# Splitting a weight tile into its two parts by DMAs in a two-block transformer kernel

## The chip, the cores and the metric

The kernel runs on one core of a Trainium2 chip. The metric is device time in microseconds, the lower the better. Below, PE is the matrix engine, DVE the vector engine, ACT the scalar engine, POOL the GpSimd engine and SP the engine that only starts DMAs and handles semaphores.

## The reference

512 tokens of width 1024 pass through two blocks in float32. The first block projects the normalised input with one wide matrix into an attention branch (8 heads, 2 key heads) and a bidirectional gated delta-rule branch (8 heads, chunks of the sequence one after the other), mixes both, and adds a gated embedding. The second block has two layers, one with stick-breaking attention and one with differential attention, each followed by a feed-forward part of width 2816:

```python
g = jnp.einsum('bsd,df->bsf', h, w_gate)
u = jnp.einsum('bsd,df->bsf', h, w_up)
return jnp.einsum('bsf,fd->bsd', jax.nn.silu(g) * u, w_down)
```

What matters here is that every weight matrix is read once and multiplied with all 512 tokens.

## The kernel before, in words

A float32 product would be slow on PE, so each operand is split into two float32r numbers: `hi`, the operand rounded to float32r, and `lo`, what is left, rounded as well. A product is then three float32r matmuls, hi by hi, hi by lo and lo by hi (`mm3`, L307). A weight tile has 128 partitions of 1024 numbers, 512 KB (768 numbers for the last third of `w_down`). It serves eight blocks of 128 rows of the reduction, so a tile is worth 24 matmuls of 512 columns (`proj_fm`, L364), or 48 of 256 columns for the projections that keep tokens on partitions (`proj_tm`, L381).

`wtile` (L322) makes the two parts. SP loads the tile into a staging buffer `st` (L327), of which there are WST = 2. ACT casts it into `whi` and DVE subtracts that from `st` into `wlo` (`split`, L317 and L320). There are WHI = 3 and WLO = 3 buffers for the parts, and from the second block on one more pair, `w3`, which every fourth tile takes (L329). A buffer comes free when PE has used its tile, a staging buffer when DVE has subtracted. In all 295 tiles go through `wtile`. 16 half tiles go another way, `wtile_big` (L335): POOL's queue loads them, and ACT and DVE split them.

The order of the work is made in two steps. A driver (L97) runs Python generators, streams such as the projections and the attention heads, against a clock of estimated times and so fixes the order in which instructions are written down. A scheduler of the framework then orders them for each engine; instructions inside `high_priority(offset=...)` (L325, offset 200) may go ahead of others by as many places. Each engine works its own queue in order, and an instruction that waits for a semaphore holds what is behind it. POOL's queue holds its arithmetic (rsqrt by a power in `small_rsqrt`, L1836, masks, clearing of tiles) and any DMA that it starts.

The rest stays as it is: two PSUM banks `acc` for the projections, five `z` for attention, one `o`.

Of the kernel before, what the change touches and what calls it, by code (L numbers as in the profile page):

```python
# [9 lines left out]
F32 = mybir.dt.float32  # L10
F32R = mybir.dt.float32r
I32 = mybir.dt.int32
AF = mybir.ActivationFunctionType
ALU = mybir.AluOpType
# [3 lines left out]
P = 128  # L18
# [29 lines left out]
CH2 = 1.3  # L48
CH3 = 1.3
INV_SLOW = 1.7  # L50
WST = 2
WHI = 3
WLO = 3
INV_LAT = 8.0
POOLS = dict(big=57, tmp=9, sm=4)
POOLS1 = dict(hf=12, lb=1)
# [23 lines left out]
class Event:  # L80
    def __init__(self):
        self.t = None
# [85 lines left out]
class Net:  # L168
    def __init__(self, ctx, tc, ins, out):
        self.tc = tc  # L170
        self.nc = tc.nc
        self.ins = ins
        self.out = out
        self.drv = Driver()
        self.pre = None
        self.nw = 0

        self.wnext = []
        self.woff = WOFF
        self.w3 = None  # L180

        self.hold = None
        pool = lambda name, bufs, **k: ctx.enter_context(tc.tile_pool(name=name, bufs=bufs, **k))
        self.cp = pool("consts", 1)
        self.wst = pool("wst", WST)
        self.whi = pool("whi", WHI)
        self.wlo = pool("wlo", WLO)
        self.xp = pool("xp", 8)
        self.dp = pool("dp", 2, space=bass.MemoryType.DRAM)
        self.ps = {"acc": pool("acc", 2, space=PSUM), "z": pool("z", 5, space=PSUM), "o": pool("o", 1, space=PSUM)}  # L190
        self.free = {"acc": Slots(2), "z": Slots(5), "o": Slots(1), "e": Slots(E_SLOTS)}
        self.preload_ln()
        self.fv = self.cp.tile([P, self.ins["fvec"].shape[1]], F32, name="fv")
        with self.tc.high_priority(offset=1000):
            self.nc.sync.dma_start(out=self.fv, in_=self.ins["fvec"])
        self.ones = self.cp.tile([P, P], F32, name="ones")
        self.nc.gpsimd.memset(self.ones, 1.0)
        self.eps1 = self.cp.tile([P, 2], F32, name="eps1")
        self.nc.gpsimd.memset(self.eps1[:, 0:1], EPS)
        self.nc.gpsimd.memset(self.eps1[:, 1:2], 4 * EPS)  # L200
        self.mhalf = self.cp.tile([P, 64], F32, name="mhalf")
        self.nc.gpsimd.memset(self.mhalf, -0.5)
        self.rfm = self.cp.tile([P, T], F32, name="rfm")
        self.rt = self.cp.tile([P, 4], F32, name="rt")
# [117 lines left out]
    def wtile(self, ap, n=1024):  # L322

        nc = self.nc
        with self.tc.high_priority(offset=self.woff):  # L325
            st = self.wst.tile([P, 1024], F32, tag="st", name="st")
            nc.sync.dma_start(out=st[:, :n], in_=ap)  # L327
            self.nw += 1
            third = self.w3 is not None and self.nw % 4 == 0  # L329
            hi = (self.w3 if third else self.whi).tile([P, 1024], F32R, tag="hi", name="whi")  # L330
            lo = (self.w3 if third else self.wlo).tile([P, 1024], F32R, tag="lo", name="wlo")
            self.split(hi[:, :n], lo[:, :n], st[:, :n])
        return hi, lo

    def wtile_big(self, ap):  # L335
# [1846 lines left out]
```

## Time and profile before

| | us |
|---|---|
| median of 3 runs (2175.8 to 2181.85) | 2178.52 |
| the profiled execution | 2179.57 |
| its span, first to last instruction | 2177.9 |
| PE busy in the span | 2101.2 |
| DVE busy | 1231.3 |
| ACT busy | 1000.5 |
| POOL busy | 117.0 |

Busy times are of one execution. Issuing a DMA isn't counted as busy. A group of instructions has a line of the code, an engine, an operation, the names of its output and inputs, a count, its busy time, the mean of one in ns, and after the bar the idle time of its engine just before, with what ended it ("issue": nothing that the profile shows). A row of DMA issues gives the size and the time from issue to landing.

### The profile page before, as it was taken

Reading aid. Unit: us, or ns where it says so; the run is one execution under the profiler, and the core shown is the slowest. Engines: PE = TensorE matmul, PEld = TensorE weight load, DVE = VectorE, ACT = ScalarE, POOL = GpSimd, SP = SyncE. Lnnn points to the kernel's source line nnn. Section 1 sums busy time; section 2 is a strip of 40 time slices with the busy share of each in tenths; the row PEclk is TensorE's granted clock in tenths of the full one; section 3 lists DMA queues with packets and bytes.
Section 4 is the critical chain, followed back from the end, with each engine's and each line's share of the span. In section 5 each row is a group of like instructions: output and inputs, shape, how many; then the busy total and the mean of one; then the engine's idle time right before and its main releaser. Section 6 shows DMA issues by size and latency. Waiting matters only on the chain.

```text
span 2177.9 us, 33391 instructions
## 1 busy us (share of the span) xinstructions
PE 2101.2 (96%) x13214; PEld 1804.9 (83%) x13214; DVE 1231.3 (57%) x2519; ACT 1000.5 (46%) x2015; POOL 117.0 (5%) x157
## 2 busy tenths in 40 slices
PE   7999999989999999899999999999999989999999
PEld 6798888879788877788878888888999878888887
DVE  8865865886542546855555444433577765444421
ACT  6556647555622355666664222222465643222211
POOL 2000110100000000000000000000111100000000
PEclk9999999999999999999999999999999999999999
DMA  4221121222334443011112222333211112333332
GB/s 154 73 81 50 46 75 50 62 78 62 103 105 142 148 153 107 14 46 59 53 45 97 97 95 95 91 95 99 88 59 51 52 54 97 97 97 96 92 110 71
DMA packets 73996, 181.72 MB, mean 83 GB/s; under 512 B 24176, under 2 KB 24816, under 8 KB 73840
## 3 DMA queue, kind: packets, MB, share of 16 engines
q1 hardware_dynamic: 72560, 175.40, 25.3%
q0 software_dynamic: 1280, 4.20, 0.6%
q8 instruction: 104, 1.70, 0.3%
q14 instruction: 52, 0.43, 0.1%
HBM read 170.13 MB, written 9.44 MB: 82 GB/s over the span
## 4 chain that ended last, share of the span: by engine, by line
PE 79%; DVE 11%; ACT 5%; issue 2%; POOL 2%; DMA 1%; SPq 0%; POOLq 0%; DVEq 0%; ACTq 0%
PE pg L301 17%; PE pd L301 11%; PE pu L301 11%; PE po L301 8%; PE pb L301 4%; PE z L301 3%; PE pv L301 3%; PE pz L301 3%; PE wS L301 2%; PE pk L301 2%; DVE wlo L320 2%; DVE cacc L845 2%; PE sb_q L301 2%; PE sb_k L301 1%; PE s L301 1%
## 5 line engine op out<-in xcount | busy, mean ns | idle before, releaser
L317 ACT CAST whi<-st 128x1024 fp32r<-128x1024 f32 (+1 forms) x295 | 305.8, 1039 | 796.1 <-issue 331.6
L320 DVE TENSOR_TENSOR wlo<-st,whi 128x1024 fp32r<-128x1024 f32 (+1 forms) x295 | 356.3, 1209 | 279.7 <-ACT whi L317 275.6
L301 PE MATMUL pg<-rlo,whi 128*128 128x512 f32 x352 | 138.7, 394 | 0.0
L301 PE MATMUL pg<-rhi,whi 128*128 128x512 f32 x352 | 138.1, 392 | 0.0
L301 PE MATMUL pg<-rhi,wlo 128*128 128x512 f32 x352 | 137.9, 392 | 0.0
L301 PE MATMUL pd<-mh,wlo 128*128 128x512 f32 x352 | 137.5, 391 | 0.0
L301 PE MATMUL pd<-mh,whi 128*128 128x512 f32 x352 | 137.5, 391 | 0.0
L301 PE MATMUL pd<-ml,whi 128*128 128x512 f32 x352 | 137.5, 391 | 0.0
L301 PE MATMUL pu<-rhi,wlo 128*128 128x512 f32 x352 | 137.2, 390 | 0.0
L301 PE MATMUL pu<-rlo,whi 128*128 128x512 f32 x352 | 137.1, 389 | 0.0
L301 PE MATMUL pu<-rhi,whi 128*128 128x512 f32 x352 | 137.0, 389 | 0.0
L2050 DVE TENSOR_TENSOR sg<-pg,rfm 128x512 f32<-128x512 f32 x44 | 30.4, 692 | 118.2 <-PE pg L301 118.1
L2056 DVE TENSOR_TENSOR m<-pu,sg 128x512 f32<-128x512 f32 x44 | 30.4, 692 | 115.4 <-PE pu L301 115.4
L301 PE MATMUL pv<-whi,rhi 128*128 128x256 f32 x256 | 75.9, 297 | 3.3 <-ACT tmq L1868 2.1
L301 PEld LDWEIGHTS pg<-rhi,wlo 128*128 128x128 f32 x352 | 66.2, 188 | 15.1 <-issue 0.5
L301 PEld LDWEIGHTS pg<-rlo,whi 128*128 128x128 f32 x352 | 66.3, 188 | 15.0 <-issue 0.5
L301 PEld LDWEIGHTS pg<-rhi,whi 128*128 128x128 f32 x352 | 66.2, 188 | 14.5
L301 PEld LDWEIGHTS pd<-ml,whi 128*128 128x128 f32 x352 | 66.2, 188 | 14.3
L301 PEld LDWEIGHTS pd<-mh,wlo 128*128 128x128 f32 x352 | 66.1, 188 | 14.3
L301 PEld LDWEIGHTS pd<-mh,whi 128*128 128x128 f32 x352 | 66.1, 188 | 14.2
L301 PEld LDWEIGHTS pu<-rhi,whi 128*128 128x128 f32 x352 | 66.1, 188 | 14.0
L301 PEld LDWEIGHTS pu<-rlo,whi 128*128 128x128 f32 x352 | 66.1, 188 | 14.0
(563 smaller groups left out, 5820.8 us busy)
## 6 DMA issues: line engine op xcount, KB each, us to landing
st<-w_gate SPq DMA_DIRECT2D x44, 512.0 KB, 3.4
st<-w_up SPq DMA_DIRECT2D x44, 512.0 KB, 3.5
st<-w_down SPq DMA_DIRECT2D x32, 512.0 KB, 3.6
st<-w_dn SPq DMA_DIRECT2D x24, 512.0 KB, 3.6
st<-w_out SPq DMA_DIRECT2D x24, 512.0 KB, 3.5
st<-w_down SPq DMA_DIRECT2D x16, 384.0 KB, 3.1
x<-xT SPq DMA_DIRECT2D x16, 256.0 KB, 6.5
st<-w_aq SPq DMA_DIRECT2D x8, 512.0 KB, 3.6
```

The costliest lines, as they stand in the source:

```text
L301: self.nc.tensor.matmul(out, lhsT=lhsT, rhs=rhs, start=start, stop=stop, skip_group_check=True)
L317: nc.scalar.copy(hi, src)
L320: nc.vector.tensor_tensor(lo, src, hi.bitcast(F32), op=ALU.subtract)
L845: nc.vector.scalar_tensor_tensor(out=acc[:, a], in0=raw[:, b], scalar=w[:, s:s + 1], in1=acc[:, a], op0=ALU.mult, op1=ALU.add)
L2050: nc.vector.tensor_tensor(sg, ps, self.rfm, op=ALU.mult)
L2056: nc.vector.tensor_tensor(m, ps, sg, op=ALU.mult)
```

## The change

The staging buffers and the load into them go. POOL's queue starts a DMA straight from DRAM into `hi`, which is float32r, so the DMA rounds. ACT then writes the negative of `hi` into `lo`, and a second DMA on POOL's queue adds the same weights from DRAM to what is in `lo`. DVE has no part in it, and SP issues no weight load of `wtile` any more. The buffers are now 4 for each part, and every fifth tile takes the extra pair in the second block.

```diff
--- before.py
+++ after.py
@@ -48,9 +48,8 @@
 CH2 = 1.3
 CH3 = 1.3
 INV_SLOW = 1.7
-WST = 2
-WHI = 3
-WLO = 3
+WHI = 4
+WLO = 4
 INV_LAT = 8.0
 POOLS = dict(big=57, tmp=9, sm=4)
 POOLS1 = dict(hf=12, lb=1)
@@ -182,7 +181,6 @@
         self.hold = None
         pool = lambda name, bufs, **k: ctx.enter_context(tc.tile_pool(name=name, bufs=bufs, **k))
         self.cp = pool("consts", 1)
-        self.wst = pool("wst", WST)
         self.whi = pool("whi", WHI)
         self.wlo = pool("wlo", WLO)
         self.xp = pool("xp", 8)
@@ -323,13 +321,14 @@
 
         nc = self.nc
         with self.tc.high_priority(offset=self.woff):
-            st = self.wst.tile([P, 1024], F32, tag="st", name="st")
-            nc.sync.dma_start(out=st[:, :n], in_=ap)
             self.nw += 1
-            third = self.w3 is not None and self.nw % 4 == 0
-            hi = (self.w3 if third else self.whi).tile([P, 1024], F32R, tag="hi", name="whi")
-            lo = (self.w3 if third else self.wlo).tile([P, 1024], F32R, tag="lo", name="wlo")
-            self.split(hi[:, :n], lo[:, :n], st[:, :n])
+            extra = self.w3 is not None and self.nw % (WHI + 1) == 0
+            hi = (self.w3 if extra else self.whi).tile([P, 1024], F32R, tag="hi", name="whi")
+            lo = (self.w3 if extra else self.wlo).tile([P, 1024], F32R, tag="lo", name="wlo")
+
+            nc.gpsimd.dma_start(out=hi[:, :n], in_=ap)
+            nc.scalar.mul(lo[:, :n], hi[:, :n].bitcast(F32), -1.0)
+            nc.gpsimd.dma_start(out=lo[:, :n], in_=ap, accum_op=ALU.add)
         return hi, lo
 
     def wtile_big(self, ap):
```

## Rows read from the trace of the kernel before

**Rows 1.** The page, busy us per engine (share of the span) and instructions

```profile
PE 2101.2 (96%) x13214; PEld 1804.9 (83%) x13214; DVE 1231.3 (57%) x2519; ACT 1000.5 (46%) x2015; POOL 117.0 (5%) x157
```

**Rows 2.** The page, the chain that ended last: by engine, by line

```profile
PE 79%; DVE 11%; ACT 5%; issue 2%; POOL 2%; DMA 1%; SPq 0%; POOLq 0%; DVEq 0%; ACTq 0%
PE pg L301 17%; PE pd L301 11%; PE pu L301 11%; PE po L301 8%; PE pb L301 4%; PE z L301 3%; PE pv L301 3%; PE pz L301 3%; PE wS L301 2%; PE pk L301 2%; DVE wlo L320 2%; DVE cacc L845 2%; PE sb_q L301 2%; PE sb_k L301 1%; PE s L301 1%
```

**Rows 3.** Windows: length, busy us of PE, PEld, DVE, ACT, POOL; clock, DMA share, GB/s

```profile
400.00:545.00 145.00, 135.11 (x1419) 122.83 (x1419) 113.88 (x285) 81.88 (x227) 9.30 (x9) 0.95 0.25 73
...
605.00:760.00 155.00, 155.00 (x689) 128.35 (x688) 62.02 (x82) 48.34 (x75) 3.30 (x4) 1.00 0.40 135
...
1170.00:1412.00 242.00, 242.00 (x1060) 198.56 (x1059) 113.75 (x138) 72.48 (x93) 0.00 (x0) 1.00 0.30 95
...
1532.00:1775.00 243.00, 224.90 (x1732) 214.65 (x1730) 177.97 (x598) 139.94 (x284) 43.76 (x41) 0.98 0.18 57
```

**Rows 4.** The chain in order of time: start, length, what

```profile
1181.53 5.44 PE pg L301 x24
```

**Rows 5.** The page, costliest groups: busy us, mean ns | idle before, releaser

```profile
L317 ACT CAST whi<-st 128x1024 fp32r<-128x1024 f32 (+1 forms) x295 | 305.8, 1039 | 796.1 <-issue 331.6
L320 DVE TENSOR_TENSOR wlo<-st,whi 128x1024 fp32r<-128x1024 f32 (+1 forms) x295 | 356.3, 1209 | 279.7 <-ACT whi L317 275.6
```

**Rows 6.** Timeline, 1230 to 1237 us: start, length, engine, line [idle before]

```profile
1230.68 1.05 ACT L317 CAST whi<-st 128x1024 fp32r<-128x1024 f32 x1 [3.87 <-issue]
...
1231.77 1.23 DVE L320 TENSOR_TENSOR wlo<-st,whi 128x1024 fp32r<-128x1024 f32 x1 [0.21 <-ACT whi L317]
...
1233.02 0.33 SPq L327 DMA_DIRECT2D st<-w_gate  x1
...
1236.12 1.05 ACT L317 CAST whi<-st 128x1024 fp32r<-128x1024 f32 x1 [3.86 <-issue]
```

**Rows 7.** Waits of SP's queue and of PE: us in total, times, longest

```profile
SPq L327 <- DVE wlo L320: 1540.9, 267, 48.9
...
PE ab L301 <- ACT whi L317: 6.7, 1, 6.7
```

**Rows 8.** The tile wbst: its loads from POOL, ns min/median/max, first and last start

```profile
L342 POOL DMA_DIRECT2D wbst<-w_ple_gate x8: 546/547/732, 754.7 to 786.9; - x8
```

**Rows 9.** POOL's groups by line: busy us, mean ns | idle before

```profile
L1839 POOL TENSOR_TENSOR rs<-ss,mhalf 128x8 f32<-128x8 f32 x8 | 15.7, 1962 | 280.6 <-DVE ss L890 280.6
```

**Rows 10.** DMA issues, 844 to 845.5 us, then 781 to 782: KB, us to landing

```profile
wbst<-sb_k POOLq DMA_DIRECT2D x1, 256.0 KB, 2.9
...
x<-xT SPq DMA_DIRECT2D x3, 256.0 KB, 7.2
wbst<-w_ple_gate POOLq DMA_DIRECT2D x1, 256.0 KB, 6.9
```

**Rows 11.** DMA queue, 1170 to 1412 us: packets, MB, share of 16 engines

```profile
q1 hardware_dynamic: 6336, 22.94, 29.5%
```

**Rows 12.** The page, DMA issues: count, KB each, median us to landing

```profile
st<-w_gate SPq DMA_DIRECT2D x44, 512.0 KB, 3.4
st<-w_up SPq DMA_DIRECT2D x44, 512.0 KB, 3.5
st<-w_down SPq DMA_DIRECT2D x32, 512.0 KB, 3.6
...
st<-w_out SPq DMA_DIRECT2D x24, 512.0 KB, 3.5
st<-w_down SPq DMA_DIRECT2D x16, 384.0 KB, 3.1
...
st<-w_ga SPq DMA_DIRECT2D x8, 512.0 KB, 3.5
...
st<-w_ple_gate SPq DMA_DIRECT2D x4, 512.0 KB, 3.5
```

**Rows 13.** The page, DMA queues over the whole span: packets, MB, share

```profile
q0 software_dynamic: 1280, 4.20, 0.6%
```

## The prediction

> **What bounds the kernel now.** I read the busy shares first. The matrix engine PE is busy for 2101.2 of 2177.9 us [rows 1], so no saving on another engine can bring more than 76.7 us, and anything that makes PE wait costs its full length. The chain that ended last says the same: 79% of it is PE, 11% DVE, 5% ACT; the step that this change takes off DVE, the subtraction that makes `wlo`, is 2% of that chain, about 44 us [rows 2].
>
> Next the stages. Two kinds alternate [rows 3]. Up to 545 us and in both attention stages PE has short gaps (135.11 of 145 us between 400 and 545; 224.90 of 243 us between 1532 and 1775) and DVE is up to 79% busy (113.88 of 145). In the long projections (605 to 760 us, 1170 to 1412, and the rest of both feed-forward blocks like it) PE is busy 100% at full granted clock, and DVE and ACT are half idle. There a weight tile of 24 matmuls is used up in 5.44 us, one tile behind the other [rows 4]. These stages set the test: the next pair `whi`, `wlo` must come at least every 5.44 us.
>
> Before, it does. `whi` takes ACT 1.04 us and `wlo` takes DVE 1.21 us [rows 5], and the steady cycle shows the slack: ACT starts the cast when a slot comes free (the next one 5.44 us later), DVE subtracts right behind it, and at the end of that SP issues the load of a later tile [rows 6]. SP's 1540.9 us of waiting is that wait for DVE [rows 7]. Load, cast and subtraction of different tiles overlap, because the load sits in a staging buffer of its own. The only wait of PE for weights that is worth naming is 6.7 us at the start [rows 7].
>
> **Part 1, work removed.** 295 subtractions of 1.21 us leave DVE, 356.3 us of its 1231.3 [rows 1, 5]. In the long projections that is worth nothing, for PE covers it all. In the stages with gaps it is worth between 0 and the 44 us above; what is late next there is the rest of DVE's and ACT's own chain, which stays, so about half would remain, 22 us. ACT's 295 casts become 295 negations of the same shape; I cost them the same 1.04 us.
>
> **Part 2, both loads go to POOL's queue.** SP's issue of 0.33 us per tile [rows 6] becomes two issues on POOL. POOL's issue of a 256 KB load takes 0.55 us [rows 8], so 1.1 us per tile, 324 us in all on an engine that is 5% busy now [rows 1]: room enough by itself. But the second DMA needs ACT's negation, which needs the first DMA, and while it waits everything behind it on POOL waits too: the first DMA of the next tile; POOL's rsqrt steps (L1839, six groups of 8, the longest of 1.96 us each, in the stages with gaps [rows 9]); its memsets; and the `wbst` loads. In those stages a late rsqrt delays DVE. I set this against the 22 us of part 1 and take 0 for both together, with ends -44 us (all gain, no wait) and +50 us (some 48 steps held 1 us each).
>
> **Part 3, the length of POOL's loop.** In the long projections slots come free one at a time, 5.44 us apart, so I expect POOL's queue to read first DMA, second DMA, next tile's first DMA, and so on. Then the loop has a fixed length: from the issue of the first to the landing, plus negation, plus the issue of the second. A 256 KB load from POOL lands after 2.9 us when little else runs [rows 10]. Another 256 KB add half of what 512 KB take on the wire: 22.94 MB are 29.5% of 242 us [rows 11], 3.11 us per MB, 1.63 us for 512 KB, 0.8 us for the half. So the landing is at 3.7 us (SP's 512 KB loads land after 3.4 to 3.6 us [rows 12]). With 1.05 us of ACT, 0.55 us for the second issue and 0.2 us allowed for the hand-overs (0.04 us from ACT to DVE in [rows 6]; none to POOL's queue is shown) the loop is 5.5 us, already no less than 5.44.
>
> That holds on idle DMA engines. They aren't idle: the adding DMA of the tile before was issued just 0.55 us ahead on the same software queue, of which there is one [rows 13]. Loads issued together do delay each other: a POOL load of 256 KB took 6.9 us beside three SP loads [rows 10]. The trace has no adding DMA. Its price on the wire lies between 1.63 us (it moves like a plain load of 512 KB) and 3.3 us (512 KB from DRAM and 512 KB from SBUF read one after the other). So the first DMA is held 1.63 - 0.55 = 1.1 us to 3.3 - 0.55 = 2.7 us, and the loop is 6.6 to 8.2 us. Below, with no delay at all, it is 5.5 us. I take 6.6 us, from the nearest row, a plain 512 KB load.
>
> The Trainium skill, page "Collectives: The Full Stack", section "The bandwidth ceiling: the fold count and why AG ≠ RS ≠ AR", holds that an add inside a DMA reads two sources through one read ring and so runs at about half the rate of a copy. By that rule the loop would be 8.2 us and the time about 2692 us (an estimate). No run here shows it yet.
>
> **The sum.** Tiles used at PE's pace: 44 + 44 + 32 + 16 of the feed-forward blocks, 24 of the output projections, four groups of 8 in the first block (`w_ga`, `w_br_att`, `w_gd`, `w_br_dn`), 4 of `w_ple_gate`: 196 [rows 12]. The other 99 are used at about 10 us each (53 of them in the first 545 us), slower than 6.6. Three stretches each begin with 4 pairs in hand: 184 tiles pay 6.6 - 5.44 = 1.16 us, 213 us. At the start the first product with `wlo` waits for a second DMA in place of a subtraction: 3.7 + 0.55 us less the 1.2, about 4 us counting what PE can do meanwhile. Parts 1 and 2: 0. The profiled execution took 2179.57 us, 1.7 us more than its span and 1.05 us above the median of 2178.52; I take that off: 2178.5 + 213 + 4 = 2396 us. With 8.2 us it is 184 x 2.76 = 508, so 2692 us; with 5.5 us 11, so 2194 us.
>
> **The rivals.** First: the order on POOL is another, the first DMA of the next tile ahead of the second DMA of this one. Then the loop may last two periods, 10.9 us, and is hidden under PE; what counts is the wire, 1.63 + 1.63 to 1.63 + 3.3 us per tile, under 5.44. PE keeps its pace and part 1's gain shows in the stages with gaps: 2157 us, 2134 at best. The point that decides: whether a slot is free for the next tile before ACT's negation of this one ends. For it: 4 pairs (5 in the second block) in place of 3 (4). Against it: slots come free only every 5.44 us, about as long as the first DMA and the negation take (4.9 us).
>
> Second: the wire. If the adding DMA takes over 5.44 - 1.63 = 3.8 us on 16 engines (2.3 times a plain load), no order helps. At 6 us a tile costs 7.6 us, 2.2 more than now, times 196: about 2610 us. For it: nothing measured; against it: DMA engines are only 30% busy [rows 11].
>
> Third: everything is hidden, and what DVE gains POOL's waits give back: 2178 us.
>
> That a DMA doesn't round as ACT's cast does would change values, not the time: the same instructions run.
>
> **Chances.** POOL's loop sets the pace: 0.55, 2396 us, its own range 2194 to 2692. The wire sets it: 0.13. Hidden with gain: 0.20. Hidden without: 0.12. A difference under 0.3% (6.5 us) can't be told from none here; so faster 0.20, same 0.12, slower 0.68. The range must take in part of the hidden cases: 2150 to 2700 us.
>
> **What would show it.** In the changed profile: matmuls `pg`, `pu`, `pd` with idle time ended by a DMA into `wlo`; POOL's second DMA waiting for ACT in nearly every tile, and its issues 6.6 us apart between two layers' matmuls; PE's share in the feed-forward stage near 5.44/6.6 = 82%; DVE's busy time about 875 us. Issues at 5.44 us with PE at 100% there prove the loop wrong, and show the first rival if the first DMAs run ahead; DMA engines busy over 90% show the second.

## The result and the profile after

The changed kernel takes 2460.48 us (median of 4 runs, 2456.69 to 2463.04) against 2178.08 for the kernel before (4 runs, 2175.80 to 2181.85): 1.129 times as long, 95% interval 1.127 to 1.132. The forecast was 2396 us, range 2150 to 2700. The profiled execution has a span of 2455.0 us, 277.1 more than before. Of the executions reported below one slow one is left out: the kernel with the rounding load alone once took 2869.81 us at a granted clock of 0.674, where its other executions had 0.98 to 0.99.

First the page of the changed kernel: busy time per engine, the chain that ended last by engine and by line, and the costliest weight group. They answer to [rows 1, 2, 5].

```profile
PE 2181.7 (89%) x13214; PEld 1846.4 (75%) x13214; DVE 895.5 (36%) x2224; ACT 1000.1 (41%) x2015; POOL 537.5 (22%) x747
...
issue 41%; PE 27%; DMA 11%; POOL 11%; ACT 5%; DVE 4%; SPq 0%; POOLq 0%; ACTq 0%; DVEq 0%
POOL whi L329 5%; POOL wlo L331 4%; PE po L299 4%; PE pz L299 2%; PE pd L299 2%; ACT wlo L330 2%; PE z L299 1%; PE pg L299 1%; PE paq L299 1%; PE pb L299 1%; DMA whi<-w_out 1%; PE pk L299 1%; PE dq L299 1%; PE wS L299 1%; PE m L299 1%
...
L330 ACT ACTIVATE wlo<-whi 128x1024 fp32r<-128x1024 f32 (+1 forms) x295 | 308.3, 1046 | 990.4 <-DMA whi<-w_down 224.9
```

DVE's busy time fell by 335.8 us, ACT's negation costs what its cast did, and PE fell from 79% of the chain to 27%. PE runs the same 13214 matmuls but is busy 80.5 us longer, with its granted clock down from 0.987 to 0.956 of full speed over the span; the other 196.6 of the 277.1 us are PE idle.

The waits of POOL and of PE in the whole span (us in total, times, longest), against [rows 7]:

```profile
POOL wlo L331 <- ACT wlo L330: 1159.8, 259, 11.6
```

```profile
PE pd L299 <- DMA wlo<-w_down: 30.6, 15, 3.8
PE pu L299 <- DVE m L2055: 29.6, 15, 3.9
PE pg L299 <- DVE sg L2049: 17.0, 10, 2.9
```

The windows of the changed kernel (length, busy us of PE, PEld, DVE, ACT, POOL; clock, DMA share, GB/s): the first stage, up to the first matmul of `w_ga` (the last chunk streams run on beside the stage behind it), the gate and up projections of the first feed-forward block, and differential attention with its output projection. Below them the same first and last stretch of the kernel before; the middle one answers to the 242 us row of [rows 3].

```profile
0.00:595.00 595.00, 524.26 (x4921) 471.16 (x4922) 339.48 (x933) 327.23 (x892) 126.28 (x176) 0.96 0.51 119
1292.70:1575.20 282.50, 254.77 (x1059) 203.46 (x1058) 63.28 (x94) 73.21 (x93) 62.22 (x87) 0.96 0.70 164
1715.00:2021.00 306.00, 265.12 (x1878) 247.01 (x1879) 162.85 (x591) 156.13 (x304) 90.74 (x106) 0.95 0.49 114
```

```profile
0.00:552.00 552.00, 514.30 (x4921) 461.81 (x4922) 397.75 (x986) 323.39 (x882) 48.26 (x65) 0.98 0.25 76
1532.00:1811.40 279.40, 261.11 (x1883) 243.89 (x1882) 200.29 (x626) 156.86 (x307) 43.76 (x41) 0.98 0.19 63
```

Gate and up of one block, 44 tiles, went from 242.1 to 282.5 us: 6.42 us per tile, where PE alone needs 5.44 at full clock. Of these 40.4 us, 12.7 are PE busy longer, at the lower clock, and 27.7 are idle. All matmuls of the kernel cut into nine stages, the growth in us is: first stage 42.8; `w_ga` to `w_br_dn` 28.5; output projection and `w_ple_gate` 27.2; stick-breaking attention with its output projection 24.8; gate and up 40.4; down 18.1; differential attention with its output projection 28.0; gate and up 39.7; down 27.6. The two feed-forward blocks, 136 tiles, are 125.8 us of it.

Why 6.42: POOL's queue in the changed kernel, 20 us of the gate and up stage (start, length, engine, line; in brackets the idle time before and who ended it).

```profile
1403.30 0.85 POOL L331 DMA_DIRECT2D wlo<-w_up  x1 [8.45 <-ACT wlo L330]
1403.85 0.87 POOL L329 DMA_DIRECT2D whi<-w_gate  x1
1404.39 0.88 POOL L329 DMA_DIRECT2D whi<-w_up  x1
1411.55 0.88 POOL L331 DMA_DIRECT2D wlo<-w_gate  x1 [6.28 <-ACT wlo L330]
1413.01 0.87 POOL L331 DMA_DIRECT2D wlo<-w_up  x1 [0.59 <-ACT wlo L330]
1413.56 0.89 POOL L329 DMA_DIRECT2D whi<-w_gate  x1
1422.44 0.85 POOL L331 DMA_DIRECT2D wlo<-w_gate  x1 [7.99 <-ACT wlo L330]
```

The second DMAs wait for ACT's negation, and in this stretch no first DMA waits for a buffer: behind a second DMA the next first ones go at once. One round trip runs from a second DMA over the first DMA behind it, its landing and the negation to the next second DMA. It takes 8.25 us from 1403.30 to 1411.55 and 9.43 us from 1413.01 to 1422.44; between them lie 1.46 us, because two first DMAs went together at 1403.85 and 1404.39 and their two second DMAs follow one another. That makes 19.14 us for three tiles, 6.38 us per tile: two of the three share a trip.

And ACT's queue with the chain from there to PE (timelines of ACT, DVE and PE, same stretch):

```profile
1410.19 1.06 ACT L330 ACTIVATE wlo<-whi 128x1024 fp32r<-128x1024 f32 x1 [6.67 <-DMA whi<-w_gate]
1411.15 0.61 ACT L2050 ACTIVATE sg<-sg 128x512 f32<-128x512 f32 x1
...
1411.80 0.69 DVE L2051 TENSOR_TENSOR sg<-sg,rfm 128x512 f32<-128x512 f32 x1 [6.96 <-ACT sg L2050]
1412.60 0.69 DVE L2055 TENSOR_TENSOR m<-pu,sg 128x512 f32<-128x512 f32 x1
...
1413.34 0.50 PE L299 MATMUL pu<-rhi,whi 128*128 128x512 f32 x1 [2.71 <-DVE m L2055]
```

PE here doesn't wait for a weight. (Such waits of `pg` and `pu` for DVE are 24.0 of the 27.7 idle us of this stage.) The silu (L2050) stands on ACT behind a negation that waits 6.67 us for a first DMA; with it wait DVE's product and the PSUM bank that PE needs next. Its weight's second DMA had been issued at 1403.30, 10 us earlier.

### The profile page after: what moved, and what is told of

It is laid out like the page before. It is cut to its first block, busy times and chain, and to the rows that moved or that the text cites. A ratio compares the mean times of both kernels' runs of the same rounds, so it can differ in the third digit from the quotient of the medians.

```text
span 2455.0 us, 33540 instructions
## 1 busy us (share of the span) xinstructions
PE 2181.7 (89%) x13214; PEld 1846.4 (75%) x13214; DVE 895.5 (36%) x2224; ACT 1000.1 (41%) x2015; POOL 537.5 (22%) x747
## 4 chain that ended last, share of the span: by engine, by line
issue 41%; PE 27%; DMA 11%; POOL 11%; ACT 5%; DVE 4%; SPq 0%; POOLq 0%; ACTq 0%; DVEq 0%
POOL whi L329 5%; POOL wlo L331 4%; PE po L299 4%; PE pz L299 2%; PE pd L299 2%; ACT wlo L330 2%; PE z L299 1%; PE pg L299 1%; PE paq L299 1%; PE pb L299 1%; DMA whi<-w_out 1%; PE pk L299 1%; PE dq L299 1%; PE wS L299 1%; PE m L299 1%
## 5 line engine op out<-in xcount | busy, mean ns | idle before, releaser
L330 ACT ACTIVATE wlo<-whi 128x1024 fp32r<-128x1024 f32 (+1 forms) x295 | 308.3, 1046 | 990.4 <-DMA whi<-w_down 224.9
L299 PE MATMUL pu<-rhi,whi 128*128 128x512 f32 x352 | 144.5, 410 | 29.6 <-DVE m L2055 29.6
L2051 DVE TENSOR_TENSOR sg<-sg,rfm 128x512 f32<-128x512 f32 x44 | 30.5, 693 | 208.5 <-ACT sg L2050 208.5
L318 DVE TENSOR_TENSOR ml<-m,mh 128x512 fp32r<-128x512 f32 x44 | 30.5, 693 | 201.7 <-ACT mh L315 201.4
L331 POOL DMA_DIRECT2D wlo<-w_down x48 | 41.7, 878 | 228.4 <-ACT wlo L330 219.7
L299 PE MATMUL pv<-whi,rhi 128*128 128x256 f32 x256 | 78.5, 306 | 12.7 <-ACT tmq L1867 12.7
L547 DVE SCALAR_TENSOR_TENSOR rlo<-x,fv,rhi 128x512 fp32r<-128x512 f32 x40 | 30.1, 752 | 161.0 <-ACT rhi L546 160.1
L331 POOL DMA_DIRECT2D wlo<-w_up x44 | 38.5, 875 | 221.9 <-ACT wlo L330 218.1
L331 POOL DMA_DIRECT2D wlo<-w_gate x44 | 38.2, 868 | 210.8 <-ACT wlo L330 203.6
L844 DVE SCALAR_TENSOR_TENSOR cacc<-craw,convw,cacc 128x510 f32<-128x510 f32 (+1 forms) x96 | 71.8, 748 | 32.6 <-ACT cacc L840 31.7
L299 PEld LDWEIGHTS pu<-rhi,wlo 128*128 128x128 f32 x352 | 68.8, 195 | 15.5
```

Source lines behind the costliest of these rows:

```text
L299: self.nc.tensor.matmul(out, lhsT=lhsT, rhs=rhs, start=start, stop=stop, skip_group_check=True)
L318: nc.vector.tensor_tensor(lo, src, hi.bitcast(F32), op=ALU.subtract)
L330: nc.scalar.mul(lo[:, :n], hi[:, :n].bitcast(F32), -1.0)
L331: nc.gpsimd.dma_start(out=lo[:, :n], in_=ap, accum_op=ALU.add)
L547: nc.vector.scalar_tensor_tensor(out=R.lo[c], in0=x, scalar=g, in1=R.hi[c].bitcast(F32), op0=ALU.mult, op1=ALU.subtract)
L844: nc.vector.scalar_tensor_tensor(out=acc[:, a], in0=raw[:, b], scalar=w[:, s:s + 1], in1=acc[:, a], op0=ALU.mult, op1=ALU.add)
```

## The experiments

Each is an edit of the kernel after or before. The theory is the loop of the prediction: POOL's queue holds the next tile's first DMA behind a second DMA that waits for the negation. Rivals are the wire and ACT's or POOL's held arithmetic.

**More first DMAs ahead.** In the kernel after:

```diff
-WHI = 4
-WLO = 4
+WHI = 5
+WLO = 3
```

With it every sixth tile, not every fifth, takes the extra pair in the second block.

> Only the sizes change: 5 buffers for the rounded part and 3 for the remainder, in place of 4 and 4; same bytes, same DMAs, same negations. The first DMA of a tile can then be issued a tile earlier, and the second DMA of a tile no longer stands behind a first DMA that has only just been issued. Theory (POOL's loop of first landing, negation, second issue sets the pace): the loop is hidden, feed-forward tiles come back to about 5.5 us, whole kernel 2170 to 2260 us. Rival (the wire sets the pace, 4.4 us of DMA engine time per pair plus contention): nothing changes, 2430 to 2480 us.

Measured 2256.6 us (4 runs, 2253.89 to 2260.26), 1.035 times before (1.032 to 1.037): the same instructions and as many bytes, 204 us less than the changed kernel. Its gate and up stage as a window:

```profile
1224.70:1467.20 242.50, 242.12 (x1060) 198.38 (x1059) 64.23 (x93) 72.80 (x93) 63.03 (x89) 1.00 0.84 191
```

Its DMA queue in that window (packets, MB, share of 16 engines), and POOL's timeline:

```profile
q0 software_dynamic: 12746, 46.18, 84.0%
```

```profile
1302.37 0.55 POOL L329 DMA_DIRECT2D whi<-w_up  x1 [3.27 <-PE pu L299]
1303.69 0.85 POOL L331 DMA_DIRECT2D wlo<-w_up  x1 [0.76 <-ACT wlo L330]
1307.87 0.55 POOL L329 DMA_DIRECT2D whi<-w_gate  x1 [3.33 <-PE pg L299]
```

Now POOL waits mostly for PE to free a buffer (113.8 us in this stage), and for ACT's negation 65.6 us where the changed kernel waits 211.4: the first DMA runs a tile ahead and the trip is hidden. PE is back at 242.1 us and full clock while the DMA engines are busier than in the changed kernel (84% against 70%). That rules out the wire as the bound of that stage. The first stage doesn't gain (600.2 us), nor does differential attention much (300.8).

**The add left out.** In the kernel after:

```diff
-            nc.gpsimd.dma_start(out=lo[:, :n], in_=ap, accum_op=ALU.add)
+            nc.gpsimd.dma_start(out=lo[:, :n], in_=ap)
```

> The second DMA doesn't add but copies (the negation before it stays, its result is overwritten, so the products are those of the weights twice); order on every queue as in the changed kernel. Measures the add's own price inside the loop. Theory: the next tile's first DMA stands behind the second one on the wire, so what a copy saves against an add (about 1.2 us per pair) comes off the loop of 6.4 us: about 5.5 us per tile, 2250 to 2350 us. Rival (only the waiting for ACT counts, what the second DMA takes on the wire doesn't): 2430 to 2470 us.

The kernel leaves out the add, so its products are those of other weights. Measured 2221.03 us (one run), below the expectation. Gate and up as a window:

```profile
1196.20:1437.90 241.70, 241.70 (x1059) 198.75 (x1058) 64.14 (x93) 73.50 (x91) 46.34 (x88) 1.00 0.58 191
```

Its DMA queue and POOL's timeline there:

```profile
q0 software_dynamic: 12679, 45.91, 58.1%
```

```profile
1302.70 0.53 POOL L331 DMA_DIRECT2D wlo<-w_gate  x1 [6.10 <-ACT wlo L330]
1303.22 0.54 POOL L329 DMA_DIRECT2D whi<-w_up  x1
1306.79 0.53 POOL L329 DMA_DIRECT2D whi<-w_gate  x1 [3.04 <-PE pu L299]
1309.49 0.53 POOL L331 DMA_DIRECT2D wlo<-w_up  x1 [2.17 <-ACT wlo L330]
```

The second DMA still waits for ACT, yet PE keeps its pace: with copies alone the trip is short enough, first DMAs even wait for buffers. So what the add takes longer than a copy, on the wire and to its landing, is what makes the loop too long. Its price: two copies take 58.1% of 241.7 us for 44 tiles, 3.19 us a pair, 1.6 each. In the changed kernel's stage the queue is busy as follows.

```profile
q0 software_dynamic: 12697, 46.07, 69.4%
```

That is 4.46 us a pair, so the add takes 2.86 us of 16 engines, 1.8 times a copy, if the load beside it keeps its 1.6. Two runs further down show each alone on this queue in the same stage: the adds (add alone, 242.2 us, SP loads), then the loads (rounding load alone, 243.3 us).

```profile
q0 software_dynamic: 6365, 23.14, 58.3%
```

```profile
q0 software_dynamic: 6337, 22.94, 28.7%
```

That is 3.2 us an add and 1.6 a load, twice as much. The Trainium skill, "Collectives: The Full Stack", section "The bandwidth ceiling: the fold count and why AG ≠ RS ≠ AR", says that the add of a collective runs at about half the rate of a copy. These traces, with 1.8 to 2.0 times the time, nearly agree.

The first stage is back as well: 555.3 us, 3.4 over before. So of its 42.8 us about 39 come with the add, and POOL's waits for ACT's negation, which stay there (126.4 us against 135.5), don't make them alone. Of the other stages with a loss only a part comes back: the output projection with `w_ple_gate` still loses 15.5 us, stick-breaking attention 11.6 and differential attention 15.8. These three, 42.9 us, make up what this kernel is longer than before (41.4 in the span).

**The negation left out too.** In the kernel after:

```diff
-            nc.scalar.mul(lo[:, :n], hi[:, :n].bitcast(F32), -1.0)
-            nc.gpsimd.dma_start(out=lo[:, :n], in_=ap, accum_op=ALU.add)
+            nc.gpsimd.dma_start(out=lo[:, :n], in_=ap)
```

> The negation and the add are left out: two copying DMAs per tile, neither waiting for ACT. Theory: POOL never waits inside a pair, no loop, PE keeps its 5.44 us per tile: 2140 to 2200 us, with what DVE gains in the stages with gaps. Rival (two issues per tile on POOL, or twice the bytes, are what costs): 2300 us or more.

The kernel leaves out the splitting itself. Measured 2164.94 us (one run). Two issues per tile on POOL and twice the bytes cost the feed-forward projections nothing (gate and up 241.7 us). ACT's 1.05 us per tile is left out here as well, so the 13 us below the kernel before (18 below the median of the runs of it that belong to this one, 2183.4) can't all be put down to DVE's missing subtractions, and they may hide a cost in other stages.

**Only in the feed-forward blocks.** The kernel before, with the three new instructions where a flag set around `ffn` is true, and the buffers of before (3 for each part and the extra pair):

```diff
+            if new:
+                nc.gpsimd.dma_start(out=hi[:, :n], in_=ap)
+                nc.scalar.mul(lo[:, :n], hi[:, :n].bitcast(F32), -1.0)
+                nc.gpsimd.dma_start(out=lo[:, :n], in_=ap, accum_op=ALU.add)
+            else:
+                self.split(hi[:, :n], lo[:, :n], st[:, :n])
```

> The change in the two feed-forward parts alone (136 tiles, with the buffers of before: 3 of each and the extra pair, the staging unused there), all else as before. Theory: the loss of those stages alone: about 40 + 18 + 40 + 28 = 126 us, 2280 to 2340 us, and the other stages within 5 us of before. Rival (what is lost is one delay passed on through the whole kernel): not the sum of its stages, 2200 us or below, or 2400 and above.

Measured 2321.66 us (one run), +141.6 in the span, all of it in the four feed-forward stages (42.9, 28.0, 43.0, 27.0); the five others changed by 0.8 us at most. The loss of those stages is made in them. The first gate and up stage as a window, and what PE waits for in it:

```profile
1169.30:1454.30 285.00, 259.50 (x1059) 207.03 (x1058) 62.99 (x92) 72.31 (x92) 61.48 (x86) 0.95 0.70 162
```

```profile
PE pg L302 <- DMA wlo<-w_gate: 16.9, 6, 3.2
PE pu L302 <- DMA wlo<-w_up: 4.5, 7, 1.0
```

The pace is 6.48 us, much as in the changed kernel, but here PE waits for the second DMA itself. The loop sets the pace, whether PE meets it at `wlo` or at a PSUM bank. What decides between the two wasn't shown; where the silu stands in ACT's queue is the likely cause.

**One part at a time.** The kernel before, with the add alone (ACT casts and negates, DVE has no part):

```diff
-            self.split(hi[:, :n], lo[:, :n], st[:, :n])
+            nc.scalar.copy(hi[:, :n], st[:, :n])
+            nc.scalar.mul(lo[:, :n], hi[:, :n].bitcast(F32), -1.0)
+            nc.gpsimd.dma_start(out=lo[:, :n], in_=ap, accum_op=ALU.add)
```

> The kernel before with the other part of the change alone: SP loads the staging buffer and ACT casts as before; DVE's subtraction is replaced by ACT's negation and POOL's adding DMA. The loop is cut: no first DMA on POOL, so none stands behind a waiting second one. Theory (the loop sets the feed-forward pace): feed-forward tiles at 5.44 us in spite of the add and of 1.05 us more of ACT per tile; whole kernel 2180 to 2270 us, what is lost lies in the stages with gaps. Rival (the add itself costs: its wait and its wire): feed-forward tiles stay above 6 us, 2380 us or more.

Measured 2230.66 us (4 runs, 2228.35 to 2236.31), 1.024 times before (1.022 to 1.026). The feed-forward stages are where they were (242.2, 120.6, 242.1, 124.5 us): with the load on SP's queue no load stands behind the waiting add, and an add alone is hidden. The loss is mainly the first stage's, 589.7 us, 37.8 more than before: PE waits there 36.7 us for adds into `wlo`, where it waited for no DMA before. The output projection with `w_ple_gate` loses 8.5 and stick-breaking attention 9.5; differential attention gains 4.4 us.

And the rounding load alone:

```diff
-            self.split(hi[:, :n], lo[:, :n], st[:, :n])
+            nc.gpsimd.dma_start(out=hi[:, :n], in_=ap)
+            nc.vector.tensor_tensor(lo[:, :n], st[:, :n], hi[:, :n].bitcast(F32), op=ALU.subtract)
```

> The kernel before with one part of the change alone: POOL's DMA rounds into the first part, SP still loads the staging buffer, DVE still subtracts; ACT's cast of the weights is gone. Twice the loads, one issue per tile on POOL, no wait for ACT on POOL. Theory: no loop, so no loss: 2150 to 2190 us. Rival (weight loads on POOL's queue cost by themselves, through late rsqrt steps and late loads): 2230 us or more.

A miss, between the two expectations: 2223.55 us (3 runs, 2213.73 to 2223.77), 1.017 times before (1.013 to 1.022). The feed-forward stages lose at most 1.2 us each; the first stage loses 17.8, `w_out` with `w_ple_gate` 8.6, differential attention 7.6. Neither part alone costs the feed-forward projections more than that, but each costs the other stages some 40 to 50 us. Only the two together on one queue make the loop.

**The negation on POOL.** In the kernel after:

```diff
-            nc.scalar.mul(lo[:, :n], hi[:, :n].bitcast(F32), -1.0)
+            nc.gpsimd.tensor_scalar(out=lo[:, :n], in0=hi[:, :n].bitcast(F32), scalar1=-1.0, scalar2=None, op0=ALU.mult)
```

> The changed kernel with the negation on POOL in place of ACT, so ACT never waits for the first DMA and nothing of ACT stands behind it. Theory for the stages with gaps: of the 43 us lost up to the first gate and the 28 us in the differential attention, most comes from ACT's own work held behind the negation that waits for the first DMA (ACT waits 80 us for such DMAs in the first stage); with the negation on POOL at least half comes back there. The feed-forward pace stays at 6.2 to 6.8 us, since the loop still holds landing, negation and issue. Whole 2390 to 2470 us. Rival (rsqrt steps held on POOL cause the loss there): these stages stay or get worse, for POOL has the negation too, 2460 to 2560 us.

2958.1 us (2953.87 to 2963.01), 1.357 times before (1.355 to 1.359), far off the expectation: POOL takes 2.80 us for what ACT does in 1.05, and the trip grows by that. The group, then the gate and up stage as a window, then POOL's timeline in it:

```profile
L330 POOL TENSOR_SCALAR wlo<-whi 128x1024 fp32r<-128x1024 f32 (+1 forms) x295 | 826.8, 2803 | 1101.7 <-DMA whi<-w_gate 206.5 <-DMA whi<-w_up 200.8 <-DMA whi<-w_down 192.2
```

```profile
1431.70:1833.60 401.90, 284.42 (x1060) 221.60 (x1059) 65.02 (x93) 31.98 (x49) 185.83 (x132) 0.86 0.52 113
```

```profile
1599.62 0.91 POOL L331 DMA_DIRECT2D wlo<-w_up  x1 [0.30 <-POOL wlo L330]
1600.21 0.88 POOL L329 DMA_DIRECT2D whi<-w_gate  x1
1606.52 2.77 POOL L330 TENSOR_SCALAR wlo<-whi 128x1024 fp32r<-128x1024 f32 x1 [5.43 <-DMA whi<-w_gate]
1609.59 0.91 POOL L331 DMA_DIRECT2D wlo<-w_gate  x1 [0.30 <-POOL wlo L330]
```

It answers another question well: no silu stands behind a negation any more, and the pace still follows the loop. A trip is 9.97 us here and, as the queue mostly alternates, brings one tile (over the stage, with a first DMA ahead in every fourth place or so, 9.13 us per tile); PE's granted clock goes down to 0.86. Whether ACT's held steps or POOL's late rsqrt cost the stages with gaps, for which it was meant, it can't tell.

**The same with 5 and 3 buffers.** Both edits above together:

> As the last, with 5 and 3 buffers. If both accounts hold (loop in the long projections, ACT held in the stages with gaps), the two gains add: 2190 to 2240 us, feed-forward tiles at 5.5 us. If POOL's own work is what is late in the stages with gaps, no better than 5 and 3 alone: 2250 us or more.

2465.73 us (one run). That is in the range of the second case, but not for its reason alone: running ahead saves 492 us, yet gate and up stay at 284.4 us, 6.46 per tile, where 5 and 3 buffers alone had brought them back to 242.5. So it doesn't settle what is late in the stages with gaps either.

**The add where it helped.** The kernel before, with the three lines of the add-alone kernel in differential attention and its output projection only:

```diff
+            net.in_diff = True
             net.diff(x, R, 1, R2)
+            net.in_diff = False
```

> The kernel before with one part of the change in one stage: in the differential attention and its output projection alone (32 tiles), DVE's subtraction is ACT's negation and POOL's add; loads and casts stay as before. With that part everywhere the stage took 274.7 us against 279.1, and the other stages lost. Theory (each stage keeps its own account, as the run with the change in the feed-forward parts alone showed): this stage 4 us shorter, the rest as before, 2172 to 2177 us, which is at the edge of what can be told. Rival (the gain there came from what the stages before had shifted): 2178 us or more.

2174.94 us (12 runs) against 2180.9 (17 runs): 0.9973 times before (0.9964 to 0.9983). The stage takes 274.9 us for 279.1, and DVE is busy 169.2 us in it for 200.3. It is the only version with the whole computation that beats both kernels, by a quarter of a per cent.

## Why the prediction was right or wrong

**The mechanism: shown.** POOL's second DMA waited for ACT 259 times of 295. Letting first DMAs run ahead takes the loss of the feed-forward projections away with the bytes unchanged; so do a shorter trip (copies) and another queue for the load (the add alone). A longer trip (negation on POOL) makes it worse.

**The loop's size: nearly right, by two errors that cancel.** 6.6 us per tile was forecast, 6.42 measured. The stretches that the sum priced outside the attention stages, 180 tiles, grew by 181.5 us in all, 1.01 us per tile against 1.16. But the trip is 8.3 to 9.4 us, not 6.6: the first DMA lands 6.3 to 7.5 us after its issue in the timelines above (median below 6.9), where 3.7 + 1.1 had been summed; behind a copy, in the kernel with copies, its median was 4.6 to 4.8. And the queue doesn't alternate strictly, as assumed: three tiles share two trips. The page's DMA issues of the changed kernel (count, KB, median us to landing), against [rows 12]:

```profile
whi<-w_gate POOLq DMA_DIRECT2D x44, 512.0 KB, 6.9
wlo<-w_gate POOLq DMA_DIRECT2D x44, 512.0 KB, 5.7
```

The add was taken at a plain load's 1.63 us, the lower of two ends; it is 2.9 to 3.2, nearer to the upper one of 3.3. With that and strict alternation the forecast for the loop would have been 7.8 to 8.2 us, too long, so that the forecast for the whole came out near by luck. (The sum for a loop of 8.2 us comes to 2690 us, not 2692.)

**PE's wait: half right.** For `pd`, idle time ends with a DMA into `wlo`, as forecast; for `pg` and `pu` with DVE. The wait is the same loop, handed on through ACT's queue. That the negation now waits for a DMA at the head of ACT's queue, with the silu behind it, stood nowhere in the sum; before, ACT's cast waited for PE to free a buffer and for its loads only 2.1 us in the whole span; now the negation waits 860 us for first DMAs. PE's share in the stage is 90%, not 82%: busy counts the slower matmuls too. The clock had no term: 80.5 us of the 277.1 are PE busy longer, and the granted clock stood at 1.00 in the gate and up stage wherever PE had no waits (before, 5 and 3 buffers, copies), at 0.96 in the changed kernel and 0.86 with the negation on POOL.

**DVE's and POOL's parts.** DVE at 895.5 us busy (forecast 875) with nothing gained. The six POOL groups of rsqrt were a small matter: DVE's waits for POOL grow only from 26.7 to 32.5 us in the first stage and from 29.5 to 34.2 in differential attention, and leaving out only the add brings the first stage back with POOL's waits for ACT still there.

**The stages with gaps: the term that was mis-sized.** Parts 1 and 2 were set at 0 with an upper end of 50 us, and the start at 4. The first stage grew by 42.8 and the two attention stages with their output projections by 24.8 and 28.0: 95.6 us. The sum left 99 tiles without any price of the loop, since one in 10 us is slower than 6.6. That is an average; a second part that lands late is late for the first product that uses it, whatever the next tile's date. The first and last matmuls of two projections in the first stage (tile view: ns min/median/max, first to last start) show where, first before, then after, then with the add left out:

```profile
L301 PE MATMUL paq<-wlo,hhi x128: 278/283/288, 93.8 to 313.3; 128*128 128x256 f32 x128
L301 PE MATMUL dk<-hhi,wlo x64: 387/389/628, 52.9 to 451.8; 128*128 128x512 f32 x64
```

```profile
L299 PE MATMUL paq<-wlo,hhi x128: 277/283/365, 108.7 to 338.1; 128*128 128x256 f32 x128
L299 PE MATMUL dk<-hhi,wlo x64: 387/389/775, 63.0 to 494.8; 128*128 128x512 f32 x64
```

```profile
L299 PE MATMUL paq<-wlo,hhi x128: 278/283/362, 97.3 to 315.7; 128*128 128x256 f32 x128
L299 PE MATMUL dk<-hhi,wlo x64: 387/389/473, 55.8 to 460.9; 128*128 128x512 f32 x64
```

The changed kernel is 10 us late at 63 us, 15 at 109, 25 at 338 and 43 at 495: a start that costs 10 to 15 us, not 4, and then a steady loss. Without the add it stays within 2.4 to 9.1 us. So the add is needed for the greater part of this loss, with POOL's loads (42.8) or SP's (37.8, the add alone); the rounding load alone loses 17.8. By which wait a late `wlo` turns into late chunk streams is open. With the add alone PE itself waits 36.7 us for DMAs in this stage, but in the changed kernel only 14.2, nearly all at the start. DVE's waits for ACT grow in this stage from 70 to 128 us, but to 110 without the add too, which loses 3.4. In the attention stages about half of the loss stays with copies (11.6 of 24.8 us and 15.8 of 28.0). It goes when the negation is left out too (3.2 and -10.8), a run that also takes the negation's work off ACT, so which of the two counts there isn't shown. Taking POOL's rsqrt to another engine was not tried.

**The rivals.** The first rival came true with 5 and 3 buffers, where the first DMAs run ahead, but for the feed-forward projections alone: the whole took 2256.6 us, not 2157; in the changed kernel they do so in one place of three only. The wire is refuted: 2.9 to 3.2 us for an add is below the 3.8 it needed. The hidden cases didn't come.

## What to carry to other kernels

Two dependent DMAs of one tile on one in-order queue make a loop: while the second waits for the compute step between them, the next tile's first can't start, and the pace is set by the length of a trip and the tiles that share one, however idle the engines are. Read the static order on the queue before pricing it, and give the first part more buffers than the second (5 and 3 here), or put the two on different queues. Both brought the feed-forward projections back here, not the first stage, and neither made the whole kernel faster than before. When a compute step becomes dependent on a fresh transfer, look at what stands behind it on its own engine: here a silu, and through it a PSUM bank.

## What the runs showed of the hardware

- A DMA that adds 512 KB from DRAM to what lies on the chip takes 1.8 to 2.0 times the wire time of a copy (2.86 us of 16 engines by subtraction, 3.2 where adds had the queue to themselves, against 1.6). In the feed-forward tiles of the changed kernel it lands after 5.5 to 5.7 us, where the copy in its place took 3.8 to 4.1.
- In the kernel with copies POOL's issue of 512 KB takes 0.53 us; in the timeline of the changed kernel shown above every issue reads 0.85 to 0.89, also a plain load's right behind an add. With 5 and 3 buffers a load that stands by itself reads 0.55, an add 0.85. Behind an issue of 0.85 us the next one started 0.55 us after it all the same.
- POOL takes 2.80 us to negate 128x1024 float32 into float32r, ACT 1.05.
- A busy wire is no bound by itself: with POOL's DMA queue busy 84% of the stage (5 and 3 buffers) PE kept full pace.
